# Two sums of weight quadrants made by accumulating transfers

## The chip, the cores and the metric

The kernel runs on one core of a Trainium2 chip. A core has five engines that work side by side, each on its own queue of instructions in order: TensorE (PE; its weight loads are listed apart as PEld), VectorE (DVE), ScalarE (ACT), GpSimd (POOL) and SyncE (SP), which does no arithmetic and issues transfers. POOL and ScalarE can issue transfers too. The metric is device time in microseconds of one execution, as the median of several runs.

## What is computed

The reference is two layers over 512 tokens of width 1024, in float32. Each layer is a mixing part and a feed-forward part, each behind a norm and added to the residual. The first layer mixes with a gated block over chunks and an attention to 256 memory tokens; the second uses an attention with a learned decay and again the memory attention. The change lies in the feed-forward part, which is the same in both layers:

```python
f = rmsnorm(h, ln_ffn_pre[layer])
f = (jax.nn.silu(f @ w_ffn_gate[layer]) * (f @ w_ffn_up[layer])) @ w_ffn_down[layer]
h = h + rmsnorm(f, ln_ffn_post[layer])
```

The hidden width is 2816, which is 22 rows of 128.

## The kernel before

**Products in parts.** A float32 operand is split into a high part (rounded to the fast format) and a low part (the rest), and a product is three products of parts, added in PSUM: high by high, low by high, high by low (`mm3`, lines 193 to 195). The split of a weight tile takes ScalarE for the high part (`A.copy`, line 241) and VectorE for the low one (line 242). The split tiles `whi` and `wlo` come from rings of eight each.

**Feed-forward.** `feed_forward` computes the first two hidden rows in the plain way, beside the boundary to the part before. The other 20 rows go in four groups (2 to 8, 8 to 14, 14 to 18, 18 to 22). In a group the rows come in pairs, and `sevens` makes for each pair of rows a gate block and an up block, each an object of `Seven`. There are 10 pairs and so 20 blocks in each layer, 40 in the kernel. After a group the down products of its rows follow (for the last group, `tail_of`).

**A block of seven products.** A block holds two rows (weights of 256 outputs) against the 512 tokens. Its weights are four quadrants of 128 x 512 elements, `a11`, `a12` (of the first row) and `a21`, `a22` (of the second). It gets both rows' results from seven products of half size in place of eight. Four sums of quadrants are needed for that, which `sums` makes on VectorE, in place where it can: `s3 = a11 + a21`, `a21 += a22`, `a11 += a21`, `a12 += a11`. Before they are overwritten, the plain `a11` and `a12` are split for two of the products. `run` issues one of the seven products, with the split of its operand; each is 12 matrix instructions of 256 columns. `end` adds the results up on VectorE and calls the code that applies the gate.

**Loads.** `loaded` (line 146) brings one weight row of 512 KB into a tile `raw` by a transfer on SyncE's queue. There are four such tiles, so two blocks' worth, shared with all other weights: a block's loads can go out when the splits of the block two before have ended. `s3` lies in one of four tiles with the tag `t`, which other temporaries share.

**What sets the order.** The program is written out in Python; a planner then orders the instructions of each engine, by a model of their times and by when their inputs and buffers come. So the sums of a block lie between other blocks' splits and end-of-block additions in VectorE's queue, and loads are issued as early as a buffer is free. All waits on semaphores follow from the accesses to tiles. POOL's queue holds a few setups, the powers of the norms (line 256) and four transfers for the memory keys of layer 1 (line 383).

Of the kernel before, what the change touches and what calls it, by code (L numbers as in the profile page):

```python
# [11 lines left out]
ALU = mybir.AluOpType  # L12
# [28 lines left out]
def hybrid(ctx: ExitStack, tc: tile.TileContext, i: dict, out: bass.AP):  # L41
    nc = tc.nc
# [11 lines left out]
    def name(s):  # L54
        n_of[s] = n_of.get(s, 0) + 1
        return f"{s}_{n_of[s]}"
# [7 lines left out]
    def prob(s, shape=(P, T)):  # L64
        return tp.tile(list(shape), F32, tag="p", name=name(s), bufs=6)

    def temp(s, shape=(P, T), tag="t", bufs=4, dt=F32):
        return tp.tile(list(shape), dt, tag=tag, name=name(s), bufs=bufs)
# [4 lines left out]
    def ps(tag, shape=(P, T), s="ps"):  # L73
        return pp.tile(list(shape), F32, tag=tag, name=name(s), bufs=2 if tag == "tr" else 3)

    V, A, PE, G = nc.vector, nc.scalar, nc.tensor, nc.gpsimd
# [66 lines left out]
    def loaded(src):  # L143

        raw = wp.tile([P, 1024], F32, tag="raw", name=name("raw"), bufs=4)
        last_load[0] = nc.sync.dma_start(raw, src)
        return raw
# [110 lines left out]
    class Norm:  # L258


        def __init__(self, width=T):
            self.r4 = small("r4")
            self.acc, self.width = None, width
# [25 lines left out]
        def sums(self, tb, cols):  # L289
            return [self.acc[:, c + tb * P : c + (tb + 1) * P] for c in range(0, T, self.width)]  # L290
# [630 lines left out]
    class Seven:  # L921
# [5 lines left out]
        def __init__(self, xs, src, tag, rows):  # L927
            self.xs, self.rows = xs, rows
            w1, w2 = loaded(src(0)), loaded(src(1))
            self.a = [w[:, d : d + 512] for w in (w1, w2) for d in (0, 512)]  # L930
            self.x, self.p = ps(tag, s="x"), ps(tag, (P, 256), s="a")
            self.q = ps(tag, (P, 256), s="e")
            self.s1, self.s2 = prob("s1"), prob("s2")
# [6 lines left out]
        def sums(self):  # L940

            a11, a12, a21, a22 = self.a
            self.s3 = temp("s3")
            V.tensor_add(self.s3, a11, a21)
            self.w1 = self.parts(a11)
            V.tensor_add(a21, a21, a22)
            self.w2 = self.parts(a12)
            V.tensor_add(a11, a21, a11)
            V.tensor_add(a12, a11, a12)
# [428 lines left out]
```

## Time and profile before

| | us |
|---|---|
| median of 3 runs | 1131.41 (1130.8 to 1132.37) |
| span of the profiled execution, first to last instruction | 1130.7 |
| TensorE busy | 1116.5 (99%) |
| VectorE busy | 893.1 (79%) |
| ScalarE busy | 662.2 (59%) |
| POOL busy | 24.7 (2%) |
| transfers on SyncE's queue | 116.05 MB, 33.1% of 16 transfer engines |
| read from HBM | 104.71 MB |

The profile is of one execution; it gives that execution's time only as the span, without what lies before its first and after its last instruction. A group row reads: line, engine, operation, what is written `<-` what is read, shape, count, then busy time in us, mean ns of one, and the idle time of the engine right before such instructions with what ended it. A row of a timeline begins with its start and its length in us; a wait follows in brackets. A row of waits reads: who waited, for whom, us in total, times, longest. A row of a transfer gives KB and the us from issue to landing. "DMA share" is the mean busy share of the 16 transfer engines. Ends of matrix instructions are modelled, and consecutive ones overlap.

### The profile page before, as it was taken

How to read it: one execution, taken by the hardware profiler on the slowest of the kernel's cores; microseconds unless marked ns; L12 is line 12 of the kernel's file. 1: busy time of each engine (PE TensorE's matmuls, PEld its weight loads, DVE VectorE, ACT ScalarE, POOL GpSimd, SP SyncE). 2: the span in 40 equal slices, each digit the busy share in tenths (PEclk: the TensorE clock that was granted, in tenths of full speed). 3: DMA queues.
4: the chain of work that ended last, by engine and by line, in shares of the span. 5: the costliest groups of instructions: out<-in, count | busy, mean ns of one | idle time of the engine just before them, and what ended most of it. 6: DMA issues, size and time to landing. Idle time of an engine off the chain costs nothing.

```text
span 1130.7 us, 19666 instructions
## 1 busy us (share of the span) xinstructions
PE 1116.5 (99%) x7470; PEld 1015.8 (90%) x7471; DVE 893.1 (79%) x1717; ACT 662.2 (59%) x1385; POOL 24.7 (2%) x42
## 2 busy tenths in 40 slices
PE   9999999999999999999999999999999999999997
PEld 6998889999899898998988898889999899898995
DVE  7878558897698587796858889958998688588775
ACT  8774468664365264476637667768765266254453
POOL 1000000000000000000000000000000000000000
PEclk9999999999999999999999999999999999999999
DMA  7513222334134223343323455521224234133222
GB/s 262 159 38 113 89 79 76 112 111 132 57 112 149 64 87 112 98 152 107 96 93 90 112 128 135 137 75 57 68 102 150 75 104 135 62 112 113 75 75 75
DMA packets 63559, 118.14 MB, mean 104 GB/s; under 512 B 5164, under 2 KB 39992, under 8 KB 63464
## 3 DMA queue, kind: packets, MB, share of 16 engines
q1 hardware_dynamic: 62584, 116.05, 33.1%
q8 instruction: 59, 0.97, 0.3%
q0 software_dynamic: 192, 0.52, 0.2%
q10 hardware_dynamic: 688, 0.31, 0.1%
q14 instruction: 36, 0.29, 0.1%
HBM read 104.71 MB, written 2.10 MB: 94 GB/s over the span
## 4 chain that ended last, share of the span: by engine, by line
PE 88%; DVE 4%; ACT 3%; issue 2%; DMA 2%; POOL 1%; SPq 0%; POOLq 0%; DVEq 0%
PE y L195 9%; PE y L194 9%; PE y L193 9%; PE a L195 5%; PE a L194 5%; PE a L193 5%; PE ps L193 4%; PE ps L195 4%; PE ps L194 4%; PE e L193 3%; PE e L195 3%; PE e L194 3%; PE x L195 3%; PE x L194 3%; PE x L193 3%
## 5 line engine op out<-in xcount | busy, mean ns | idle before, releaser
L241 ACT CAST whi<-raw 128x512 fp32r<-128x512 f32 x460 | 276.7, 620 | 271.4 <-PE y L195 111.3
L242 DVE TENSOR_TENSOR wlo<-raw,whi 128x512 fp32r<-128x512 f32 x460 | 305.6, 685 | 113.2 <-ACT whi L241 109.2
L193 PE MATMUL y<-whi,fhi 128*128 128x512 f32 (+1 forms) x356 | 138.5, 390 | 0.9 <-DVE s L983 0.6
L194 PE MATMUL y<-wlo,fhi 128*128 128x512 f32 (+1 forms) x356 | 138.0, 388 | 0.3 <-DVE wlo L242 0.3
L195 PE MATMUL y<-whi,flo 128*128 128x512 f32 (+1 forms) x356 | 138.1, 388 | 0.1
L193 PE MATMUL x<-xshi,whi 128*128 128x256 f32 x320 | 90.6, 283 | 0.0
L194 PE MATMUL x<-xslo,whi 128*128 128x256 f32 x320 | 90.6, 283 | 0.0
L195 PE MATMUL x<-xshi,wlo 128*128 128x256 f32 x320 | 90.6, 283 | 0.0
L194 PE MATMUL a<-xslo,whi 128*128 128x256 f32 x320 | 90.5, 283 | 0.0
L193 PE MATMUL a<-xshi,whi 128*128 128x256 f32 x320 | 90.5, 283 | 0.0
L195 PE MATMUL a<-xshi,wlo 128*128 128x256 f32 x320 | 90.4, 283 | 0.0
L193 PEld LDWEIGHTS y<-whi,fhi 128*128 128x128 f32 x356 | 66.9, 188 | 15.4 <-DVE s L983 1.3
L195 PEld LDWEIGHTS y<-whi,flo 128*128 128x128 f32 x356 | 66.9, 188 | 14.6 <-DVE flo L242 1.1
L194 PEld LDWEIGHTS y<-wlo,fhi 128*128 128x128 f32 x356 | 66.9, 188 | 14.3 <-DVE wlo L242 1.2
L193 PE MATMUL ps<-xshi,whi 128*128 128x256 f32 (+1 forms) x224 | 67.8, 305 | 0.0
L195 PE MATMUL ps<-xshi,wlo 128*128 128x256 f32 (+1 forms) x224 | 66.8, 300 | 0.0
L194 PE MATMUL ps<-xslo,whi 128*128 128x256 f32 (+1 forms) x224 | 66.2, 298 | 0.0
L193 PEld LDWEIGHTS a<-xshi,whi 128*128 128x128 f32 x320 | 61.4, 192 | 0.3
L194 PEld LDWEIGHTS a<-xslo,whi 128*128 128x128 f32 x320 | 61.4, 192 | 0.3
L193 PEld LDWEIGHTS x<-xshi,whi 128*128 128x128 f32 x320 | 61.4, 192 | 0.0
L194 PEld LDWEIGHTS x<-xslo,whi 128*128 128x128 f32 x320 | 61.4, 192 | 0.0
L195 PEld LDWEIGHTS x<-xshi,wlo 128*128 128x128 f32 x320 | 61.4, 192 | 0.0
(292 smaller groups left out, 3115.6 us busy)
## 6 DMA issues: line engine op xcount, KB each, us to landing
raw<-in_w_gate SPq DMA_DIRECT2D x44, 512.0 KB, 4.2
raw<-in_w_up SPq DMA_DIRECT2D x44, 512.0 KB, 3.5
raw<-in_w_down SPq DMA_DIRECT2D x44, 512.0 KB, 3.7
raw<-in_w_out SPq DMA_DIRECT2D x16, 512.0 KB, 4.7
raw<-in_w_b_q SPq DMA_DIRECT2D x8, 512.0 KB, 3.5
raw<-in_w_a_v SPq DMA_DIRECT2D x6, 512.0 KB, 6.4
raw<-in_w_a_u SPq DMA_DIRECT2D x6, 512.0 KB
raw<-in_w_v SPq DMA_DIRECT2D x6, 512.0 KB, 3.4
```

Of the source, the lines that this page charges most:

```text
L193: PE.matmul(o, w[0], x[0], start=start, stop=False, skip_group_check=more)
L194: PE.matmul(o, w[0], x[1], start=False, stop=False, skip_group_check=more)
L195: return PE.matmul(o, w[1], x[0], start=False, stop=stop, skip_group_check=more)
L241: A.copy(hi, src)
L242: (eng or V).tensor_sub(lo, src, hi)
```

## The change

The sum `s3` and the sum `a21 += a22` are no longer made by VectorE. When a block is set up, SyncE loads `a21` a second time, into the tile of `s3`; POOL then issues a transfer that adds `a22`, read again from HBM, to the `a21` of the loaded weights in SBUF, and one that adds `a11`, read again from HBM, to `s3`. Each of the three moves 128 x 512 elements, 256 KB. [...] The third and fourth sum stay on VectorE and read the accumulated `a21`. `s3` now takes its tile when the block is set up, ahead of the sums.

```diff
             self.xs, self.rows = xs, rows
             w1, w2 = loaded(src(0)), loaded(src(1))
             self.a = [w[:, d : d + 512] for w in (w1, w2) for d in (0, 512)]
+            self.s3 = temp("s3")
+            nc.sync.dma_start(self.s3, src(1)[:, :512])
+            G.dma_start(w2[:, :512], src(1)[:, 512:], accum_op=ALU.add)
+            G.dma_start(self.s3, src(0)[:, :512], accum_op=ALU.add)
             self.x, self.p = ps(tag, s="x"), ps(tag, (P, 256), s="a")
...
         def sums(self):
 
             a11, a12, a21, a22 = self.a
-            self.s3 = temp("s3")
-            V.tensor_add(self.s3, a11, a21)
             self.w1 = self.parts(a11)
-            V.tensor_add(a21, a21, a22)
             self.w2 = self.parts(a12)
             V.tensor_add(a11, a21, a11)
             V.tensor_add(a12, a11, a12)
```

## The prediction

> **What bounds the kernel now.** I read the page's totals first, then the busy time in stretches, then TensorE's waits, and last the timelines of the places where the changed sums stand.
>
> ```profile
> span 1130.7 us, 19666 instructions
> ...
> PE 1116.5 (99%) x7470; PEld 1015.8 (90%) x7471; DVE 893.1 (79%) x1717; ACT 662.2 (59%) x1385; POOL 24.7 (2%) x42
> ...
> L946 DVE TENSOR_TENSOR raw<-raw 128x512 f32<-128x512 f32 x40 | 27.4, 685 | 0.3
> L944 DVE TENSOR_TENSOR s<-raw,raw 128x512 f32<-128x512 f32 x40 | 27.4, 685 | 10.1 <-DMA raw<-in_w_gate 10.0
> ```
>
> TensorE is busy for 1116.5 of 1130.7 us, so 14.2 us are all that any edit off TensorE could give back. The two groups that the change deletes are 80 VectorE additions, 54.8 us busy. What they are worth is read from the stage in which they stand. The stretches below (four of layer 0; the sum is over these and the four of layer 1) are the seven-product blocks, 40 in all; a stretch runs from its first product to its last.
>
> ```profile
> core 0: us, PE busy (x) PEld busy (x) DVE busy (x) ACT busy (x) POOL busy (x), PEclk, DMA share, GB/s
> 208.80:269.20 60.40, 60.40 (x504) 60.36 (x504) 56.49 (x101) 39.64 (x81) 0.00 (x0) 1.00 0.37 121
> 302.00:362.40 60.40, 60.40 (x505) 60.40 (x504) 54.31 (x93) 37.11 (x75) 0.00 (x0) 1.00 0.36 115
> 395.10:435.40 40.30, 40.30 (x337) 40.27 (x336) 34.56 (x59) 24.37 (x49) 0.00 (x0) 1.00 0.38 119
> 458.50:498.70 40.20, 40.20 (x336) 40.19 (x335) 36.35 (x66) 26.75 (x57) 0.00 (x0) 1.00 0.31 100
> ...
> sum 402.50, PE 402.50 PEld 402.37 DVE 359.88 ACT 251.56 POOL 0.00; mean PE 50.31 PEld 50.30 DVE 44.98 ACT 31.45 POOL 0.00
> ```
>
> TensorE is busy for 402.50 of 402.50 us at a granted clock of 1.00. VectorE is busy for 359.88, so it is close behind (89%, and 94% in the opening stretch), but TensorE never waits for it here. The waits say the same for the whole kernel:
>
> ```profile
> PE y L193 <- DVE s L983: 0.6, 1, 0.6
> ...
> DVE s L944 <- DMA raw<-in_w_gate: 10.0, 8, 2.7
> ...
> SPq L146 <- DVE wlo L242: 428.9, 72, 29.0
> ```
>
> The first row is the one wait of TensorE that comes out of this stage (a product right behind a stretch, which waited for an end-of-block addition). The second is VectorE standing at the first deleted addition for a load; the third says that SyncE hangs on a free weight buffer nearly all the time: a block's loads go out when the splits of the block two before it have ended.
>
> **The change, part by part.**
>
> *Removed.* 40 L944 and 40 L946. By the sum row they lie wholly beside TensorE work, so their 54.8 us give TensorE nothing. What goes from the path is at most that 0.6 us wait, which stands behind an L944 held by its load:
>
> ```profile
> 436.49 0.69 DVE L944 TENSOR_TENSOR s<-raw,raw 128x512 f32<-128x512 f32 x1 [1.07 <-DMA raw<-in_w_gate]
> ...
> 438.30 0.50 PE L193 MATMUL y<-whi,fhi 128*128 128x512 f32 x1 [0.63 <-DVE s L983]
> ```
>
> Gain: 0 to 0.6 us; I take 0.3. Late next behind it would be the same products' own splits.
>
> *SyncE's queue.* 40 more plain loads of 256 KB, behind each block's two. Each issue costs SyncE what the loads beside it cost, 0.33 us in most rows below and 1.2 us from one issue to the next; queued behind are the next block's loads, which wait for a buffer for 428.9 us in total anyway. Cost 0.
>
> *POOL's queue.* 80 accumulating transfers, each held until the load it adds to has landed. The only transfers that POOL issues before are these four:
>
> ```profile
> L383 POOL DMA_DIRECT2D memk<-memk x4: 522/523/726, 506.6 to 508.4; - x4
> ...
> DMA to landing us min/median/max: 3.0/3.3/3.7
> ...
> 505.62 1.78 DVE L381 TENSOR_TENSOR memk<-memk,memk 64x256 fp32r<-64x256 f32 x4
> ...
> 177.61 1.55 SPq L146 DMA_DIRECT2D raw<-in_w_gate  x2
> ...
> 184.82 0.99 POOL L256 TENSOR_TENSOR r<-var,mhalf 128x2 f32<-128x2 f32 x1 [11.91 <-ACT hs L859]
> ```
>
> An issue there took 0.52 to 0.73 us for 64 partitions; for 128 I take twice the upper, 1.5 us: 80 x 1.5 = 120 us on an engine that is idle all through the stretches. VectorE's additions beside those issues ran at 0.45 us each (four in 1.78), so an issue does not hold VectorE: 0. Behind POOL's waits stand only the powers of the norms (the last row); the first block's second load goes out at 178.8 (0.33 before its row ends) and, landing within 5 us, lets the accumulate go at 183.8, before that power. If a power did stand behind an accumulate, it would be late by one landing, once in a layer: 0 to 5 us; I take 0, since the planner places instructions by when their inputs come.
>
> *The transfers themselves.* No transfer here accumulates, so I bound one. Below: a row that moves as much or less, 3.0 us to landing. Above: the longest load, 8.9 us.
>
> ```profile
> raw<-in_w_a_q SPq DMA_DIRECT2D x2, 256.0 KB, 3.0
> ...
> DMA to landing us min/median/max: 3.0/3.7/8.9
> ...
> q1 hardware_dynamic: 62584, 116.05, 33.1%
> ```
>
> I take the two reads one behind the other, 3.0 from memory and 3.3 within the chip: 6.3 us. In engine time, the queue's row gives 116.05 MB in 0.331 x 16 x 1130.7 us, 19.4 GB/s per engine, so 310 GB/s on 16 engines; a 256 KB copy is 0.85 us of all engines. Each block of 10.08 us (60.40 / 6) gains one plain copy, 0.08 of the share, and two accumulates, 0.17 if they go at a copy's rate: 0.37 becomes 0.62. [...] From the copies alone, the engines fill when an accumulate costs (1 - 0.37 - 0.08) x 10.08 / 2 = 2.8 us of all engines, 3.3 times a copy.
>
> *The new wait.* The third sum (L948) and the product of s3 now need the accumulate, behind the load. What counts is the time between a block's second load and its L948. I worked that out for all 40 blocks. It is shortest at the third block of each layer, and 10 us or more elsewhere; the rows are the third block, one between, and an ordinary one:
>
> ```profile
> 813.70 1.53 SPq L146 DMA_DIRECT2D raw<-in_w_gate  x2
> ...
> 821.63 0.68 DVE L948 TENSOR_TENSOR raw<-raw,raw 128x512 f32<-128x512 f32 x1
> ...
> 216.15 1.56 SPq L146 DMA_DIRECT2D raw<-in_w_gate  x2
> ...
> 222.32 0.69 DVE L944 TENSOR_TENSOR s<-raw,raw 128x512 f32<-128x512 f32 x1 [1.17 <-DMA raw<-in_w_gate]
> ...
> 224.73 0.69 DVE L948 TENSOR_TENSOR raw<-raw,raw 128x512 f32<-128x512 f32 x1
> ...
> 233.32 0.28 PE L193 MATMUL a<-d2hi,whi 128*128 128x256 f32 x1
> ...
> 431.57 4.83 DMA raw<-in_w_gate
> ...
> 442.37 0.68 DVE L948 TENSOR_TENSOR raw<-raw,raw 128x512 f32<-128x512 f32 x1
> ...
> 320.84 1.65 SPq L146 DMA_DIRECT2D raw<-in_w_gate  x2
> ...
> 336.80 0.68 DVE L948 TENSOR_TENSOR raw<-raw,raw 128x512 f32<-128x512 f32 x1
> ...
> 342.30 0.28 PE L193 MATMUL a<-xshi,whi 128*128 128x256 f32 x1
> ```
>
> The second load goes out one issue before the end of its row (217.4, 322.2). A load of 4.8 us and an accumulate of 6.3 make 11.1 us. In an ordinary block L948 stands 14.6 us behind the load and the block's first product 20.1: hidden by 3.5 and more. At 431.57 it stands 10.8 behind, but that block's first product only comes at 458.5, where the next stretch begins. In the third block the load lands at 222.3, the accumulate at 228.6, and L948 with its split (0.69 + 0.62 for ScalarE's half + 0.68) ends by 230.6. TensorE takes that product at 233.32. So the data are in time by 2.7 us; the accumulate may take 9.0 us there before TensorE has to wait, and the upper bound is 8.9.
>
> **Sum**: 1130.7 - 0.3 + 0 = 1130.4 for the profiled execution. The runs' median is 1131.41, 0.7 above that span, so 1131.1.
>
> **The rivals.**
>
> *Opening stall (slower).* VectorE works in order. If the third block's L948 keeps its place in the queue, VectorE stands there until 228.6, 3.9 us after 224.73; two additions deleted behind it give 1.2 back, and the split for the next product but one shows how little lead there is:
>
> ```profile
> 233.40 0.68 DVE L242 TENSOR_TENSOR wlo<-raw,whi 128x512 fp32r<-128x512 f32 x1
> ...
> 234.76 0.28 PE L193 MATMUL e<-t,whi 128*128 128x256 f32 x1
> ```
>
> It ends 0.7 us ahead of its product. So TensorE would lose 3.9 - 1.2 - 0.7 = 2.0 us per layer, 4 in both: 1135. At an accumulate of 8.9 us it is 2 x 4.6: 1140. It decides once the accumulate takes over 4.3 us and L948 is not moved back. For it: this stretch is VectorE's fullest (94%). Against it: in 40 blocks VectorE waited for a load 8 times, 2.7 us at most, so the plan puts readers about where their data come; and six deleted additions ahead of that place leave room to move other work forward.
>
> *Transfers become the bound (slower).* Above 3.3 copies' worth an accumulate fills the engines. At four (3.4 us) a block needs 0.45 x 10.08 + 6.8 = 11.3 us, 1.2 over 10.08; in 40 blocks 50 us: 1181. For it: no row here shows what an addition in a transfer costs. Against it: it takes over three times a copy's time, and the share now is 0.37.
>
> *Faster.* VectorE falls from 89% to 76% of the stretches ((359.9 - 54.8) / 402.5), and a gain over 0.2% would need 2.3 us of TensorE's idle time. The stretches have none and the only wait beside them is 0.6 us: 1130.8 at best, so this counts only if the new plan also removes waits elsewhere, about 1129.
>
> **How the numbers follow.** 0.2% (2.3 us) is about what can be told from no change here. Hidden, 1131.1: 0.52, with a range of its own of 1130 to 1133. Opening stall, 1135 to 1140: 0.28. Transfers the bound, 1150 and over: 0.16. Faster: 0.04. The same holds the first, slower the next two, so 0.04, 0.52 and 0.44. The range goes from 1130 to 1145: it leaves out the case of full transfer engines and the gain, 0.20.
>
> **What would show it.** Right: VectorE's busy time lower by about 50 us, TensorE still busy throughout the stretches, L948 waiting for an accumulate now and then without TensorE behind it, landings of 4 to 7 us, DMA share 0.6 to 0.8. Wrong: TensorE idle in the third block of a layer (opening stall); TensorE idle in every block, share near 1, landings far over 9 us (full engines); the powers of the norms late behind POOL's transfers.

## The result, and the profile after

The changed kernel takes 1146.78 us as the median of four runs (1144.74 to 1147.7); the kernel before takes 1131.11 us beside it (four runs, 1130.09 to 1132.37). The ratio is 1.0133, with a 95% interval of 1.0118 to 1.0147: slower by about 15 us. The profiled execution of the changed kernel is its quickest run, 1144.74 us with a span of 1143.0, so its trace shows 12.3 us of the loss.

First the page of the changed kernel: span, busy times, transfer queues, HBM, and one row of transfers (KB and us to landing).

```profile
span 1143.0 us, 19973 instructions
...
PE 1119.2 (98%) x7471; PEld 1017.5 (89%) x7471; DVE 849.5 (74%) x1637; ACT 661.7 (58%) x1385; POOL 93.8 (8%) x122
...
q1 hardware_dynamic: 68344, 126.53, 36.3%
q0 software_dynamic: 11712, 21.50, 11.6%
...
HBM read 136.16 MB, written 2.10 MB: 121 GB/s over the span
...
raw<-in_w_gate POOLq DMA_DIRECT2D x20, 256.0 KB, 4.4
```

The change did what it says: exactly 80 VectorE instructions are gone, POOL issues 80 more, and 31.45 MB more come from HBM. VectorE is busy for 43.6 us less. Yet the span is 12.3 us longer, with TensorE busy for only 2.7 us more. So most of the loss, 9.6 us, is TensorE standing idle: 23.8 us in all, where 14.2 were idle before.

Next the stretches of the changed kernel (columns as in the prediction): the opening stretch of layer 0 from its first product to its last, a later stretch, and the opening stretch of layer 1.

```profile
core 0: us, PE busy (x) PEld busy (x) DVE busy (x) ACT busy (x) POOL busy (x), PEclk, DMA share, GB/s
208.80:274.00 65.20, 62.23 (x509) 61.42 (x508) 50.95 (x88) 39.48 (x82) 10.29 (x13) 1.00 0.81 206
302.00:362.40 60.40, 60.40 (x487) 59.58 (x486) 49.31 (x83) 35.60 (x73) 7.69 (x9) 1.00 0.65 166
806.10:875.70 69.60, 67.97 (x534) 66.14 (x533) 56.98 (x101) 42.87 (x89) 11.98 (x14) 1.00 0.78 195
```

The stretch from 302.0 is as full as before: TensorE busy for 60.40 of 60.40 us. In the opening stretches TensorE is idle for 3.0 and 1.6 us, though VectorE has less to do. The waits name the places. Here are those of TensorE that are new, and those of VectorE at the third sum, which is L949 in the changed kernel (L948 before).

```profile
DVE raw L949 <- DMA raw<-in_w_gate: 10.3, 2, 5.8
...
DVE raw L949 <- issue: 5.7, 2, 3.0
PE y L195 <- DVE flo L242: 5.6, 2, 2.9
...
DVE raw L949 <- DMA raw<-in_w_up: 4.3, 2, 2.4
...
PE a L193 <- ACT s L975: 2.4, 2, 2.2
...
PE e L193 <- ACT s L978: 1.2, 2, 0.6
...
PE a L193 <- DVE s L983: 1.0, 1, 1.0
```

VectorE stands at the third sum six times, for 20.3 us. By the timeline they are three blocks of each layer: the third (5.83 and 4.44 us), the sixth (2.40 and 1.93) and the seventeenth, the first block of the last group (3.01 and 2.67). TensorE has a new gap right behind the third block's sum (2.2 and 1.0 us) and behind the seventeenth's (2.9 and 2.6), and next to none behind the sixth's (0.2 in layer 0). Two more gaps of 0.6 (the row with L978) lie about 20 us after the third block's sum. There ScalarE waited for VectorE's end-of-block work, and no reader stood waiting for a transfer; why that work came late there wasn't followed up. These six gaps, without the one of 0.2, make 10.0 us.

The third block of layer 0 step by step. The chain of waits of the changed kernel shows it (start, us, what; "issue" is time for which the profile names no releaser):

```profile
217.81 5.40 DMA raw<-in_w_gate
223.28 0.48 issue
223.77 5.11 DMA raw<-in_w_gate
228.96 0.70 DVE raw L949
229.85 0.44 issue
230.29 0.38 ACT s L975
230.71 0.39 PE a L193
```

The load lands after 5.40 us, POOL issues the accumulate, this lands after 5.11, and only then does VectorE start the third sum. The last three rows show what TensorE waits for. It isn't the product of this sum, which comes later. It is a copy by ScalarE (L975) that empties the PSUM tile for `a`, and that copy has nothing to do with this sum. Why it is late stands in the timelines of VectorE, ScalarE and TensorE at the place:

```profile
228.96 0.69 DVE L949 TENSOR_TENSOR raw<-raw,raw 128x512 f32<-128x512 f32 x1 [5.83 <-DMA raw<-in_w_gate]
...
229.76 0.62 ACT L241 CAST whi<-raw 128x512 fp32r<-128x512 f32 x1 [6.16 <-DVE raw L949]
230.29 0.37 ACT L975 COPY s<-a 128x256 f32<-128x256 f32 x1
...
230.71 0.39 PE L193 MATMUL a<-xshi,whi 128*128 128x256 f32 x1 [2.16 <-ACT s L975]
```

At the head of ScalarE's queue stood the high part of the third sum, for 6.16 us up to 229.76, and behind it stood the copy, which began at 230.29. So here one late transfer stops two engines, and TensorE starves through the second. In layer 1 the path is shorter: there TensorE waits for an end-of-block addition that stands behind the sum in VectorE's own queue (1.0 us, the row with L983).

The seventeenth block of layer 0. VectorE and TensorE of the changed kernel:

```profile
444.37 0.69 DVE L242 TENSOR_TENSOR flo<-s,fhi 128x512 fp32r<-128x512 f32 x1
448.06 0.69 DVE L949 TENSOR_TENSOR raw<-raw,raw 128x512 f32<-128x512 f32 x1 [3.01 <-issue]
448.67 0.68 DVE L242 TENSOR_TENSOR flo<-s,fhi 128x512 fp32r<-128x512 f32 x1
...
449.40 0.50 PE L195 MATMUL y<-whi,flo 128*128 128x512 f32 x1 [2.94 <-DVE flo L242]
```

The third sum stands between the two low splits (`flo`) of the last hidden rows of the group. The down products that run at that moment need the second of them, and TensorE waits 2.94 us. In the kernel before, the sum at 442.37, shown in the prediction, stood behind both:

```profile
441.77 0.68 DVE L242 TENSOR_TENSOR flo<-s,fhi 128x512 fp32r<-128x512 f32 x1
```

The profile gives "issue" as the releaser of that wait of 3.01 us, that is nothing it could name. The transfer row names it: the accumulate of this block went out at 442.16, and it took this long to land (the answer for line L933 between 442 and 443 us):

```profile
L933 POOL DMA_DIRECT2D raw<-in_w_gate x1: 847/847/847, 442.2 to 442.2; - x1
...
DMA to landing us min/median/max: 5.8/5.8/5.8
```

442.16 and 5.8 are 447.96, and the sum begins at 448.06. In layer 1 it is the same: 6.4 us from 1042.9, and the sum at 1049.42.

What is left is 2.7 us of TensorE's busy time. Part of it is a stretch at half clock behind the last of the gaps:

```profile
1052.10:1055.50 3.40, 3.40 (x10) 2.63 (x9) 0.94 (x2) 0.62 (x1) 0.00 (x0) 0.50 0.33 57
```

The granted clock is 0.50 for 3.4 us, and products of 512 columns begin 0.43 us apart there, 0.23 before it. That costs about half of the 3.4, 1.7 us. The gaps (10.0 us) and this make 11.7 of the 12.3 us. The other three runs took 1.7 to 3.0 us longer at a mean granted clock of 0.995, against 0.998 in the profiled one; more time at half clock would fit that, but they have no trace to show it.

### The profile page after: what moved, and what is told of

It is laid out like the page before. It is cut to its first block, busy times and chain, and to the rows that moved or that the text cites. A ratio compares the mean times of both kernels' runs of the same rounds, so it can differ in the third digit from the quotient of the medians.

```text
span 1143.0 us, 19973 instructions
## 1 busy us (share of the span) xinstructions
PE 1119.2 (98%) x7471; PEld 1017.5 (89%) x7471; DVE 849.5 (74%) x1637; ACT 661.7 (58%) x1385; POOL 93.8 (8%) x122
## 3 DMA queue, kind: packets, MB, share of 16 engines
q0 software_dynamic: 11712, 21.50, 11.6%
## 4 chain that ended last, share of the span: by engine, by line
PE 81%; DMA 5%; DVE 5%; issue 4%; ACT 4%; POOL 1%; POOLq 0%; SPq 0%; DVEq 0%; ACTq 0%
PE y L195 8%; PE y L194 8%; PE y L193 8%; PE a L193 4%; PE a L194 4%; PE a L195 4%; PE ps L193 4%; PE ps L195 4%; PE ps L194 4%; DMA raw<-in_w_gate 3%; PE e L193 3%; PE x L195 3%; PE x L194 3%; PE x L193 3%; PE e L195 3%
```

## The experiments

Three theories stood at the start:

- **W, the wait**: VectorE (and ScalarE with it) stands in order at the third sum until the accumulate into the loaded weights has landed, and other blocks' work stands behind it.
- **L, the load on the transfer engines**: the added traffic itself makes weight loads late, whoever reads the sums.
- **R, the order**: with the sums gone the planner lays all engines out in another way, and that order is worse.

In three sessions the kernel before took 1131.61, 1131.26 and 1131.03 us. Ratios are against it; each interval is 95%. Each edit is shown against the changed kernel, where nothing else is said; `...` stands for lines left out.

### Only s3 accumulated

```diff
-            G.dma_start(w2[:, :512], src(1)[:, 512:], accum_op=ALU.add)
...
             self.w1 = self.parts(a11)
+            V.tensor_add(a21, a21, a22)
             self.w2 = self.parts(a12)
```

> Only s3 is made by an accumulating transfer; the sum of a21 and a22 is back on VectorE, so the third sum waits for a plain load as before. Theory W (VectorE's queue, which is in order, stands at the third sum until the accumulate into the loaded weights has landed, in the third block of each layer and ahead of the last group): the four long waits of the third sum (5.8, 4.4, 3.0, 2.7 us) go, and the time is 1131 to 1134 us. Theory L (the transfer engines are loaded so much that all landings are late): half of the accumulates are left, so about half of the loss, 1137 to 1140 us. Theory R (the loss comes from the planner's other order once additions are gone): half of the additions are gone, somewhere between 1134 and 1147 us.

Measured: 1132.06 us, ratio 1.0002 (0.9993 to 1.0011). The 40 accumulates into `s3`, with their 40 extra loads, cost nothing that can be measured, though they are the ones that take longer to land (median 5.7 us against 4.2 in the changed kernel). They start early, in tiles of their own: counted in order, the accumulate for the third block goes out at 208.59, and ScalarE splits the sum at 222.26. In the whole run ScalarE waits for one of them once, for 0.4 us. This speaks for W.

### Only a21 accumulated

`s3` is made by VectorE from the second load of `a21`, which stays.

```diff
-            G.dma_start(self.s3, src(0)[:, :512], accum_op=ALU.add)
...
             a11, a12, a21, a22 = self.a
+            V.tensor_add(self.s3, self.s3, a11)
```

> Only the sum of a21 and a22 is made by an accumulating transfer; s3 is loaded with a21 as in the change, and VectorE adds a11 to it, so 40 accumulates are left. Theory W (VectorE's queue stands at the third sum until the accumulate into the loaded weights has landed): the waits stay, and so does most of the loss, 1139 to 1147 us. Theory L (loaded transfer engines): as with s3 alone, where nothing was lost, 1131 to 1134 us.

Measured: 1143.73 us, ratio 1.0112 (1.0097 to 1.0127). So the 40 accumulates into `a21` carry most of the loss by themselves. The waits of this run show the group's end again, with TensorE's two gaps at 1.64 and 3.62 us:

```profile
DVE raw L949 <- issue: 10.0, 4, 3.7
...
PE y L195 <- DVE flo L242: 5.3, 2, 3.6
```

By the timeline, the four waits of the first row are the seventeenth blocks (1.70 and 3.68 us) and the third blocks (2.26 and 2.40, where the changed kernel waits 5.83 and 4.44). So with half of the accumulates the opening's waits are shorter, but not gone; VectorE also stands at the `s3` additions here, for loads (12.2 us in all).

### The same traffic on the kernel before, read by nobody

Two loads and two accumulates more for each block, into two spare tiles; the sums stay as before. This edit is against the kernel before.

```diff
             self.a = [w[:, d : d + 512] for w in (w1, w2) for d in (0, 512)]
+            for s in range(2):
+                spare = temp("spare", tag="acc", bufs=2)
+                nc.sync.dma_start(spare, src(1)[:, :512])
+                G.dma_start(spare, src(s)[:, 512 * s : 512 * s + 512], accum_op=ALU.add)
```

> The kernel before, with all four sums on VectorE, and beside them per block two plain loads and two accumulating transfers of 256 KB into two spare tiles that nobody reads: as many accumulates as in the change and one plain load more per block. Theory W: nobody waits for them, 1131 to 1133 us. Theory L: the same load on the engines makes weights late, 1143 to 1150 us. Theory R: no addition is gone, 1131 to 1133 us.

Measured: 1247.39 us, ratio 1.1019 (1.1001 to 1.1037), far off what either theory gives. As a test of traffic it failed, since it made waits of its own. Its waits:

```profile
PE yt L799 <- ACT y L792: 39.6, 6, 13.9
...
PE y L193 <- ACT whi L241: 20.4, 2, 19.8
...
PE rb L252 <- POOL r L256: 10.2, 4, 5.7
```

With only two spare tiles each load into one waits on SyncE for the accumulate two before it (153 and 137 us of SyncE's waits are at those loads), and weight loads stand behind it. POOL's accumulates wait for these loads (134.7 and 131.9 us), and the powers of the norms, which also run on POOL, stand behind them: the last row, and behind it the first. That is the mechanism of W on two other queues. It doesn't tell W from L.

### The sum in a tile of its own

`a21 + a22` is accumulated in a third tile, so that the loaded weights stay untouched and the load and its accumulate have a buffer that is free early. The sixth product (`what == 5`) reads the loaded `a21` here instead of the sum, so this kernel computes something else there, with the same work.

```diff
-            G.dma_start(w2[:, :512], src(1)[:, 512:], accum_op=ALU.add)
+            self.sum = temp("sum", tag="acc", bufs=2)
+            nc.sync.dma_start(self.sum, src(1)[:, :512])
+            G.dma_start(self.sum, src(1)[:, 512:], accum_op=ALU.add)
...
-            V.tensor_add(a11, a21, a11)
+            V.tensor_add(a11, self.sum, a11)
```

> Both sums stay accumulates, but the sum of a21 and a22 gets a tile of its own (two of them, free of the four weight buffers), loaded and accumulated up to two blocks ahead, so that the third sum finds it ready. VectorE has the same 80 additions less as in the change, and there are 10 MB more of plain loads. Theory W: the third sum's waits go, 1131 to 1135 us. Theory L: more traffic than the change has, 1147 us or more. Theory R: the same additions are gone, about 1146 us.

Measured: 1134.44 us, ratio 1.0024 (1.0013 to 1.0034), with still more traffic than the change. Most of the loss is gone. One gap of 3.6 us remains in the opening stretch of layer 0; a row of the chain of waits there, and one of TensorE's waits:

```profile
215.31 11.08 DMA raw<-in_w_gate
```

```profile
PE e L193 <- ACT s L980: 3.6, 1, 3.6
```

Here the first load of the third block held the chain for 11.08 us, where 8.9 was the longest landing before. The second took 9.9, and 5.40 in the changed kernel. The 11.08 us run from this load's issue, and no accumulate writes into its tile in this kernel. So the author's estimate is that the larger burst at the opening is the reason, and that L has a share in this kernel; no run takes that apart.

### Both sums left out, no accumulates

The second load of `a21` stays; `s3` and `a21` are used without their second term.

```diff
-            G.dma_start(w2[:, :512], src(1)[:, 512:], accum_op=ALU.add)
-            G.dma_start(self.s3, src(0)[:, :512], accum_op=ALU.add)
```

> The change without its 80 accumulating transfers: the two sums are left out of the computation, a21 stays as loaded and s3 holds a21. VectorE has the same 80 additions less; the plain load of s3 stays. Theory W: no accumulate to wait for, 1130 to 1132 us. Theory L: a third of the added traffic, and none of the slow kind, 1131 to 1134 us. Theory R: the order that the planner finds without the additions is the cause, about 1146 us.

Measured: 1129.61 us, ratio 0.9983 (0.9974 to 0.9992). R as stated falls: the plan without the 80 additions is no worse. It is 1.9 us better, and that is what the freed VectorE time was worth in this run. In this kernel too the third sum stands between the two low splits at the group's end, and doesn't wait:

```profile
439.61 0.69 DVE L242 TENSOR_TENSOR flo<-s,fhi 128x512 fp32r<-128x512 f32 x1
440.21 0.68 DVE L947 TENSOR_TENSOR raw<-raw,raw 128x512 f32<-128x512 f32 x1
440.81 0.69 DVE L242 TENSOR_TENSOR flo<-s,fhi 128x512 fp32r<-128x512 f32 x1
```

So the place alone costs nothing; what costs there is the place and a late transfer together.

### Plain copies in place of the accumulates

POOL issues the same 80 transfers, but they overwrite. The sums are thus left out.

```diff
-            G.dma_start(w2[:, :512], src(1)[:, 512:], accum_op=ALU.add)
-            G.dma_start(self.s3, src(0)[:, :512], accum_op=ALU.add)
+            G.dma_start(w2[:, :512], src(1)[:, 512:])
+            G.dma_start(self.s3, src(0)[:, :512])
```

> The change with both accumulating transfers turned into plain copies on POOL's queue from and to the same places, so the two sums are left out (a21 becomes a22, s3 becomes a11), while the order of load, second transfer and third sum stays. [...] Theory W in the form that the second transfer behind the load is what costs, whatever it does: 1138 to 1146 us. If the slowness of adding in a transfer costs (an accumulate moved 10.1 GB/s per engine, a copy 19): 1131 to 1134 us.

Measured: 1137.28 us, ratio 1.0058 (1.0043 to 1.0073). About 6 of the 15 us stay when the second transfer is a plain copy. Its queue on the page, and, from the answer for line L933, the landing of the copies into the loaded weights:

```profile
q0 software_dynamic: 6592, 21.50, 6.1%
```

```profile
DMA to landing us min/median/max: 2.9/3.2/5.5
```

The same 21.50 MB take 6.1% of the engines' span instead of 11.6%, and land in 3.2 us at the median where the accumulates take 4.2 (3.9 to 6.4). So here a reader that waits for two transfers in a row costs about 6 us even when the second lands in 3.2; that it adds makes the loss more than twice as large.

### Accumulates that nobody reads, started when the weights are there

As without accumulates, and 80 accumulates into two spare tiles, each let go by a one-column copy on VectorE. The sums are left out.

```diff
+            for s, (w, more) in enumerate(zip((a21, a22), self.more)):
+                V.tensor_copy(spares[s][:, :1], w[:, :1])
+                G.dma_start(spares[s], more, accum_op=ALU.add)
```

> All 80 accumulating transfers with their sources, but into two spare tiles that nobody reads; each starts behind its block's second load, by a copy of one column on VectorE into the spare tile. The two sums are left out, as in the run without accumulates (1129.6 us). Theory W: nobody waits for an accumulate, 1130 to 1132 us. Theory L: the engines carry the same accumulates, 1140 to 1147 us.

Measured: 1146.01 us, ratio 1.0134 (1.0117 to 1.0151), as slow as the change. This doesn't decide, because the small copies waited themselves, each for the accumulate before it into the same tile:

```profile
DVE spare L949 <- DMA spare<-in_w_gate: 30.5, 17, 6.0
...
PE a L193 <- DVE s L987: 5.7, 2, 3.3
```

An instruction of one column that stands for up to 6 us at the head of VectorE's queue could be the cause, but the traffic was there as well.

### The addition back on VectorE in six of the forty blocks

The sum `a21` is made by VectorE in the three blocks of each layer in which the third sum waited (third, sixth, seventeenth); 74 of the 80 accumulates stay.

```diff
+            self.n = made[0] % 20
+            made[0] += 1
+            if self.n not in (2, 5, 16):
+                G.dma_start(w2[:, :512], src(1)[:, 512:], accum_op=ALU.add)
...
+            if self.n in (2, 5, 16):
+                V.tensor_add(a21, a21, a22)
```

> The change, but in the six blocks whose third sum waited longest (in each layer the third, the sixth and the seventeenth) VectorE makes the sum of a21 and a22 again; 74 of 80 accumulates are left. Theory W: the loss goes, 1131 to 1134 us. Theory L: 74/80 of the load is left, 1144 to 1147 us.

Measured: 1131.61 us, ratio 1.0001 (0.9991 to 1.0011): the whole loss is gone. The traffic is not. The stretches of this run:

```profile
208.80:269.20 60.40, 59.69 (x492) 59.25 (x491) 51.07 (x90) 39.23 (x81) 9.61 (x12) 1.00 0.80 208
302.00:362.40 60.40, 60.40 (x497) 60.01 (x496) 50.41 (x85) 36.78 (x75) 7.69 (x9) 1.00 0.68 174
```

The opening stretch takes 60.40 us again at a DMA share of 0.80 (0.81 in the changed kernel), and the accumulates into the loaded weights that remain land in 4.0 to 6.8 us, where 3.9 to 6.4 were measured in the changed kernel. This decides between W and L: the transfer engines at that share cost nothing that can be measured, once the sums at these places need no accumulate. One other third sum in the opening stretch still waits for its transfer, for 2.94 us up to 247.54, about as long as those of the seventeenth blocks in the changed kernel, and TensorE stands for only 0.71 us there. So the length of a wait is not its price.

### The two places apart

First only the seventeenth blocks get their addition back (so the waits at the opening stay), then only the third and sixth (so those at the group's end stay). The edits are that of the last experiment with other lists:

```diff
-            if self.n not in (2, 5, 16):
+            if self.n not in (16,):
```

and in the second kernel

```diff
-            if self.n not in (2, 5, 16):
+            if self.n not in (2, 5):
```

The first:

> The change with the sum of a21 and a22 back on VectorE only in the seventeenth block of each layer (the first of the last group). If the loss is the sum of separate places, what stays is that of the third and sixth blocks: in the trace of the change the products of the sixth block end 4.8 us later in layer 0, and the same stretch adds 2.5 us in layer 1, so 1137 to 1140 us. If the places are one chain, so that the later one follows from the lateness of the opening: no change, about 1146 us, or all of it gone, 1132 us.

Measured: 1139.72 us, ratio 1.0075 (1.0057 to 1.0093). The waits of this run:

```profile
DVE raw L956 <- DMA raw<-in_w_gate: 9.8, 2, 5.1
...
PE a L193 <- ACT s L982: 3.4, 1, 3.4
```

The second:

> The reverse: the sum is back on VectorE only in the third and sixth block of each layer; the seventeenth still takes an accumulate. If the places add up, what stays is the wait ahead of the last group (2.9 and 2.6 us of TensorE, with the half clock behind one of them): 1137 to 1141 us, and this and the run before lose together what the change loses, about 15 us.

Measured: 1140.53 us, ratio 1.0080 (1.0065 to 1.0096). The waits of this run:

```profile
DVE raw L956 <- issue: 5.6, 2, 3.1
PE y L195 <- DVE flo L242: 5.5, 2, 3.1
```

Each place has its own wait of TensorE and about half of the loss. Together 0.75% and 0.80% make 1.55%, against 1.33% (1.18 to 1.47) for the change: they add up roughly, a little beyond. The sixth block was not tested apart from the third.

### The third sum held behind the last low split

All 80 accumulates stay. Only in the seventeenth blocks the third sum may not be issued before the last `flo` split of the group before.

```diff
-            V.tensor_add(a11, a21, a11)
+            if self.n == 16:
+                with tc.issue_after(last_low[0].ins):
+                    V.tensor_add(a11, a21, a11)
+            else:
+                V.tensor_add(a11, a21, a11)
...
-            split(u, *fs[len(fs) - 2 + row])
+            last_low[0] = split(u, *fs[len(fs) - 2 + row])
```

> All 80 accumulates as in the change; in the seventeenth block of each layer the third sum is held in VectorE's queue behind the last split of the group before, which stood behind it. If the place in VectorE's queue is what costs there, TensorE's waits of 2.9 and 2.6 us for that split go and the time is that of the run with the opening left, 1137 to 1141 us. If the accumulate itself is too late for the products, the waits stay or move to that block's own products, 1145 us or more.

Measured: 1138.38 us, ratio 1.0059 (1.0041 to 1.0077). VectorE at the place, in this run:

```profile
446.33 1.28 DVE L242 TENSOR_TENSOR flo<-s,fhi 128x512 fp32r<-128x512 f32 x2
449.90 0.69 DVE L955 TENSOR_TENSOR raw<-raw,raw 128x512 f32<-128x512 f32 x1 [2.29 <-issue]
```

VectorE waits 2.29 us as ever, but both low splits are already done, and TensorE's wait for `flo` is gone from the list. About 8 us are won back by moving one instruction past one other in each layer, with every transfer in place. What stays is the opening (3.4 us of TensorE's waiting at L975's copy in layer 0).

No kernel here that makes all the sums is faster than the kernel before. The two best of them (only `s3` accumulated, and the addition back in six blocks) equal it.

## Why the prediction was wrong

The forecast was 1131.1 us, no change; measured were 1146.78, beyond the range's end of 1145 and beyond the 1135 to 1140 of the opening stall.

**The chain of two transfers was sized right as a whole.** The load of 4.8 us and the accumulate of 6.3, 11.1 in all, were in the third block of layer 0 5.40, 0.48 and 5.11 (11.15 from the load at 217.81 to the sum at 228.96, where the prediction had the data at 228.6). That the whole agrees so closely is luck: the load was longer and the accumulate shorter. In the seventeenth it is 11.8, from the load at 436.30 to the sum at 448.06, with 5.8 for the accumulate. All accumulates of the changed kernel land within the bounds of 3.0 to 8.9: 3.9 to 6.4 into the weights, 3.7 to 8.9 into `s3`.

**The step that failed is the third block's slack.** "So the data are in time by 2.7 us" compared the landing with the moment at which TensorE takes the product of that very sum. The landing was as forecast, and TensorE stopped anyway, from 228.55 to 230.71, for a copy that stood behind the sum's high split on ScalarE. The product of the sum came only at 236.57 (233.32 in the kernel before), long after its data. What was to be priced was not when the product of L948 is due but what stands behind L948 and behind its split in the queues of VectorE and ScalarE. The prediction asked that of POOL's and SyncE's queues, and of VectorE's only in the rival; of ScalarE's nowhere.

**The same step, worse, for the seventeenth block.** The prediction saw that L948 "stands 10.8 behind" there, less than the 11.1 that it had just worked out, and called it hidden as that block's products come only at 458.5. Behind the sum stood the low split for down products that run at that moment. This place alone costs 0.80%, and no rival had it.

**"The plan puts readers about where their data come"** was taken from waits of 2.7 us at most. In the changed kernel the third sum waits for up to 5.83 us, and at the group's end it was put ahead of a split that it had stood behind. How the planner prices an accumulate wasn't looked into.

**The rival "opening stall"** had the right start, VectorE standing at the third sum, and for its place about the right size: 2.0 us a layer worked out, 2.8 and 1.6 us of gaps measured in the opening stretches. Its condition (over 4.3 us, and L948 not moved back) was met: the accumulate took 5.11. Its path to TensorE was another: it went by the lead of the low splits on VectorE, where the trace of layer 0 shows ScalarE's copy. What it lacked is the group's end, 2.9 and 2.6 us, and the half clock behind a gap, 1.7. In the run with only the opening left the loss is 8.7 us, with a gap of 3.4 us in layer 0 and a mean granted clock of 0.996 in its profiled execution (0.999 in the kernel before), so that place can cost twice the 4 us that the rival worked out for both layers.

**The rival "transfers become the bound"** is refuted by the run with six additions back, where the loss is gone at a DMA share of 0.80 in the opening stretch. In the changed kernel the share is 0.81 in that stretch, the fullest of the three shown; around the third block's wait, from 214 to 229 us, it is 0.99 (0.43 before). An accumulate takes 0.116 x 1143.0 us / 80, so 1.66 us of all 16 engines, against 0.87 for a plain copy in the run with copies (0.061 x 1137.3 / 80; forecast 0.85; both with the four small transfers of line 383 left in): 1.9 copies, where 3.3 would fill the engines by the prediction's reckoning. The forecast of "0.6 to 0.8" for the share had 0.62 at a copy's rate; its upper end was the author's estimate, and no run shows the cost of an accumulate that it took. What the runs showed is the 1.66 us: with it a block gives 0.37 + 0.08 + 2 x 1.66 / 10.08 = 0.78, which fits the opening stretches (0.81 and 0.78). The stretch from 302.0 (0.65) is near 0.62 for another reason: only 9 of POOL's transfers went out in it, where the prediction reckoned with 12.

**Right**: SyncE's 40 extra loads cost nothing (the run without accumulates has them, at 1129.61). POOL's issues were bounded at 1.5 us each and took 0.86, beside other work. The powers of the norms are hardly late in the changed kernel (TensorE waits for them for 1.5 us, 0.9 before); that they can be is shown by the 10.2 us in the run with unread traffic. The case of a gain was put at about 1129, and the run without accumulates, which has the freed VectorE time and no new wait, gives 1129.61.

**VectorE's busy time** fell by 43.6 us, not by the 54.8 of the two groups. Neighbouring rows begin 0.60 us apart and last 0.68 each (439.61, 440.21 and 440.81 in the run without accumulates), so a group's sum counts the overlap twice and the engine's total doesn't: 43.6 / 80 is 0.55.

## What to carry to other kernels

An operation that is taken off an engine and made by a transfer can leave a wait in the queue of each engine that reads the result: here, at the third block, 5.83 us on VectorE, and 6.16 on ScalarE, which reads next. Price it by what stands behind the first reader, on that engine and on the engine that reads next, at the time when the data come; the moment when the result itself is needed doesn't tell it. Look at the few places where the load is late and the queue holds work that the bound engine needs soon: here six of forty blocks carried the whole loss, and putting their additions back, with 74 of the 80 accumulates left, removed it.

## What the runs showed of the hardware

The granted TensorE clock fell to 0.50 for 3.4 us from 1052.1, behind the gap of 2.61 us at 1048.2, but not behind the one of 2.94 us at 446.5 in the same run (1.00 from 444 to 452 us). So such a gap may cost 4.3 us, as an estimate from the 2.61 and half of the 3.4 behind it. Behind the gap of 3.6 us in the run with the sum in a tile of its own, the products of 256 columns take 0.21 us each in the chain of waits from 228.24 on, where they take 0.12 in the changed kernel's. The mean granted clock of a profiled execution was 0.999 in the kernel before and with six additions back, 0.998 in the change and with unread accumulates (TensorE's longest gap 3.3 us), 0.997 with plain copies (2.0), with only `a21` accumulated (3.6) and with the third sum behind the split (3.4), and 0.996 with only the opening left (3.4) and with only the group's end left (3.1); a mean doesn't say behind which gap the clock was lower.

In these runs a transfer that adds took the engines 1.9 times what a plain copy of the same bytes took (1.66 against 0.87 us), and landed about 1 us later (at the median 4.2 against 3.2 into the loaded weights, 5.7 against 4.5 into `s3`). POOL was held by 0.86 us for each issue, where a plain copy held it for 0.54.
